# Loading a merge's inverse blocks ahead of its other inputs, in a fused attention and DeltaNet layer

## The chip, the cores and the metric

The kernel runs on one core of a Trainium2 chip. The metric is the time of one execution on the device in microseconds (us). Inside the core, TensorE (PE) multiplies matrices and transposes, VectorE (DVE), ScalarE (ACT) and GpSimd (POOL) work elementwise, and SyncE (SP) issues most transfers between the chip's memory and the on-chip buffers. Each engine takes its instructions strictly in program order; they meet at semaphores.

## The reference, cut to what matters

One layer of a diffusion backbone mixes 1024 latent tokens (and 256 context tokens) in two ways side by side: neighbourhood attention with 8 heads, and a bidirectional gated DeltaNet with 4 heads. The change is in the DeltaNet's preparation. For each chunk of tokens and each direction it needs the inverse of a unit triangular matrix:

```python
a = jnp.where(pos[:, None] > pos[None, :],
              jnp.einsum('nbhid,nbhjd->nbhij', kb, k) * decay, 0.0)
t_inv = lax.linalg.triangular_solve(eye + a, jnp.broadcast_to(eye, a.shape),
                                    left_side=True, lower=True, unit_diagonal=True)
u = jnp.einsum('nbhij,nbhje->nbhie', t_inv, v * beta[..., None])
```

The inverses are then used in a scan over the chunks. The kernel uses chunks of 128 tokens, so 10 chunks (2 context, 8 latent), 2 directions and 4 heads: 80 triangular matrices of 128 x 128.

## The kernel before, in words

The kernel has two phases. In the first (to about 552 us), all projections of the inputs run on TensorE, with the preparation of the DeltaNet spread among them; in the second, attention and the scan run interleaved, and then the output projection.

**Inverting in blocks.** A 128 x 128 triangular matrix is cut into four diagonal blocks of 32. For each head, `delta_front` computes the triangular matrices (`pm`), stores them to memory (`pm_dram`, one tensor per head), and copies their diagonal blocks, from memory to memory, to `ab_dram` (line 1046), one block per row. `inv_groups` loads 120 such rows at a time (the last group, number 2, has 80: line 1055, tile `ab_vv`), and `inv_blocks` inverts them on VectorE in 31 steps of two instructions (lines 1078 and 1081). The inverted blocks go back to memory as `yd` (line 1087). Groups 0 and 1 hold heads 0, 1 and most of head 2; group 2 holds the rest of head 2 and head 3.

**Merging.** `inv_merge` puts one head's inverse together, in turns that are separated by `yield`:

- turn l: load `pm` of the head (two loads `pmf`, one per direction, line 1095), and the inverted blocks (four loads `vl`, line 1106, 20 rows each);
- turn t: three VectorE transposes, `vx`, `vd`, `ld` (lines 1114 to 1116), and four ScalarE copies into `tm` (line 1120);
- turn z: 40 small matmuls `tz` of `pmf` and `ld` (line 1128), ScalarE copies `zt` (line 1132), more copies into `xo` and `tm`;
- turn u: 60 small matmuls `tu` (line 1147) and six VectorE copies (line 1152);
- turns w and e: the same once more for blocks of 64 (lines 1161 to 1172), and the store of the result `tm` to `tm_dram` (line 1174).

The turns of the four heads follow the list `MERGES`, "0l 0t 1l 0z 0u 1t 0w 2l 0e ...". Two buffers `vl` serve heads 0, 2 and heads 1, 3; `pmf` too has one pair of buffers for the even heads (in the pool `pf`, tags `kk0`, `kk1`) and one for the odd. `tm` has one buffer per parity for direction 0, and one, `tms[2]`, that all heads share for direction 1.

**What sets the order.** A scheduler orders each engine's instructions from the program's order, priorities and dependencies. `phase_a2` takes turns between the remaining projections (`self.fill`) and two generators: `blocks`, which inverts group 2 and then loads the attention's first inputs, and `merges`. Turns of `merges` run with the priority raised by 200, the first turn of `blocks` by 300. `self.order(r, name)` adds a pure order between two instructions.

**SyncE's ring.** Each transfer that SyncE issues takes one of eight semaphores in turn, and waits for the transfer that used it last, eight places earlier. While a transfer waits, everything behind it in SyncE's queue waits too.

**Projections.** They have three PSUM buffers, taken in turn. A result is split by ScalarE and VectorE into a high and a low part (`sh`, `sl`, lines 527 to 531), which are stored to `qk_dram` from a ring of four buffers (lines 532, 533). In the listings, `pk2_1` is the second half of k of the third pair of attention heads, `pz2_0` a half of its gate, `pq3_0` a half of q of the fourth pair.

Of the kernel before, what the change touches and what calls it, by code (L numbers as in the profile page):

```python
# [11 lines left out]
F32 = mybir.dt.float32  # L12
# [8 lines left out]
P = 128  # L21
# [120 lines left out]
class K:  # L142
# [946 lines left out]
    def inv_merge(self, g3, ps, h):  # L1089
        nc = self.nc  # L1090
        pm = []
        for d in range(2):
            pool, tag = (g3, f"pm{d}") if h % 2 else (self.pf, f"kk{d}")
            pm.append(pool.tile([P, 10, P], F32, name=f"pmf{h}_{d}", tag=tag))
            nc.sync.dma_start(pm[d][0:96], self.pm_dram[h][0:96, d])
        if h == 0:

            self.vls = [self.pf.tile([P, S], F32, name=f"vl{i}", tag=f"q{c}") for i, c in enumerate(("l0", "h1"))]
# [4 lines left out]
        vl = self.vls[h % 2]  # L1103
        for b in range(4):
            g, i = divmod(8 * h + 2 * b, 12)
            nc.sync.dma_start(vl[32 * b:32 * b + 20], self.yd[g][10 * i:10 * i + 20].rearrange("t j i -> t (j i)"))
        vd, ld = (g3.tile([P, 2, 10, 32], F32, name=f"{c}d{h}", tag=f"{c}d", bufs=2) for c in "vl")

        xo = self.xo
        tm = [self.tms[h % 2], self.tms[2]]  # L1110
        yield
        vx = self.pf.tile([P, S], F32, name=f"vx{h}", tag="ql1")
        flat = lambda w: w.rearrange("p d t c -> p (d t c)")
        nc.vector.transpose(vx, vl)
# [25 lines left out]
        for d in range(2):  # L1140
            pu = ps.tile([P, 10, 32], F32, name=f"tu{h}_{d}", tag="tb", bufs=2)
            where = [(r, r + c - 1) for r in (1, 3) for c in (0, 1) if (r, c) != ((3, 1), (1, 0))[d]]
            for t in range(10):
                for r, c in where:
                    s2, sc = slice(32 * r, 32 * r + 32), slice(32 * c, 32 * c + 32)
                    a, b = (zt, vd) if c < r else (vd, zt)
# [293 lines left out]
    def phase_a2(self):  # L1440
        tc, ps = self.tc, self.ps
        with tc.tile_pool(name="a2", bufs=1, side="right", reuse_waits="tile") as ap:
            ready = self.ready
            buf = lambda nm, tag, n: self.pf.tile([P, n], F32, name=f"{nm}_{tag}", tag=tag)

            def blocks():
                vv = buf("ab", "vv", 2 * S)
                yield from self.inv_groups((2,), lambda nm, n: buf("tb2", "qh0", n) if n < S else vv[:, :S] if "ab" in nm
                                           else vv[:, S:])
                self.mk = self.pf.tile([P, MTOT], mybir.dt.bfloat16, name="mk")  # L1450
                self.load(self.mk, self.I["masks"])
                while len(ready) < 4:
                    yield
                self.na_pairs = {0: self.na_load(None, 0)}
                yield

            def merges():

                heads = [self.inv_merge(ap, ps, h) for h in range(4)]
                for c in MERGES.split():  # L1460
                    h = int(c[0])
                    while c[1:] == "l" and (8 * h + 7) // 12 not in self.yd:
                        yield
                    next(heads[h])
                    if c[1:] == "e":
                        ready.append(h)
                    yield

            pr, gens = self.fill, (blocks(), merges())
            credit = [0.0, 0.0]  # L1470
            first = True
            for _ in range(3):
                next(pr)
            for _ in pr:
                for i, (g, r) in enumerate(zip(gens, (3, 3))):
                    credit[i] += r
                    while credit[i] > 0:
                        if i:
                            with tc.high_priority(offset=200):
                                next(g, None)  # L1480
                        elif first:
                            first = False
                            with tc.high_priority(offset=300):
                                next(g, None)
                        else:
                            next(g, None)
                        credit[i] -= 1
            for g in gens:
                for _ in g:
                    pass  # L1490
# [66 lines left out]
```

## Time and profile before

| | before |
|---|---|
| median of 3 runs | 872.3 us (871.33 to 875.08) |
| profiled execution, its time | 871.71 us |
| its span, first to last instruction | 869.9 us |
| mean granted clock of TensorE | 0.972 |
| PE busy | 824.9 us, 95% of the span |
| DVE busy | 502.7 us, 58% |
| ACT busy | 417.3 us, 48% |
| POOL busy | 357.3 us, 41% |
| SyncE's and ScalarE's transfers (q1, hardware queue) | 144.94 MB, 53% of the 16 engines' span |

How to read it: all times are counted from the first instruction of the span. A row of the timeline has the start, the length, the engine, the line, the operation, `out<-in` by the program's names (heads and buffer numbers left out, so `vl` is either buffer and `pmf` any head's), and in brackets the idle time of the engine just before it with what ended it. "SPq" rows are the issuing of transfers; their length is the time of issue, not of the transfer. In a row of stretches, PE's busy share counts time at a low clock as busy, so the granted clock stands beside it. Matmuls overlap in the pipeline: their pitch is read from their starts.

### The profile page before, as it was taken

To read this page: it belongs to the slowest core of one execution; us is meant where nothing else is said; L and a number is where in the kernel's file an instruction comes from. 1 tells how busy PE (TensorE), PEld (TensorE's weight loads), DVE (VectorE), ACT (ScalarE), POOL (GpSimd) and SP (SyncE) were. 2 spreads that over 40 slices of the span, in tenths; PEclk is the share of its full clock that TensorE was granted. 3 is DMA by queue.
4 is the path that set the end of the run, shared out by engine and by line. 5 is a ranking of instruction groups with operands and counts; after the bars stand their busy time and mean duration, and the time that the engine had idled before them with its cause. 6 is when DMAs were issued, how large, how long until landed. Compare 5 with 4: busy or idle time off the path is not lost.

```text
span 869.9 us, 16461 instructions
## 1 busy us (share of the span) xinstructions
PE 824.9 (95%) x6082; PEld 696.4 (80%) x6082; DVE 502.7 (58%) x1051; ACT 417.3 (48%) x1087; POOL 357.3 (41%) x430
## 2 busy tenths in 40 slices
PE   6999999999999989989898999899999999999996
PEld 3678887888788867769786788788898988878885
DVE  3444455536743699859935964456666655653342
ACT  5244334753664643355314334366666667734210
POOL 2224141453462553328262100655757559624110
PEclk9999999999999999989998999699999999999999
DMA  8778352255444825562597569995967925134251
GB/s 340 265 259 295 97 170 88 73 170 168 142 157 154 221 85 170 176 171 81 176 283 226 160 187 290 419 258 149 313 179 262 259 78 191 49 110 133 87 184 69
DMA packets 86054, 159.65 MB, mean 184 GB/s; under 512 B 18373, under 2 KB 45334, under 8 KB 83798
## 3 DMA queue, kind: packets, MB, share of 16 engines
q1 hardware_dynamic: 78486, 144.94, 53.0%
q10 hardware_dynamic: 7488, 13.67, 5.1%
q8 instruction: 48, 0.79, 0.4%
q14 instruction: 32, 0.26, 0.1%
HBM read 109.51 MB, written 52.42 MB: 186 GB/s over the span
## 4 chain that ended last, share of the span: by engine, by line
PE 59%; DVE 16%; DMA 15%; issue 4%; ACT 2%; POOL 2%; SPq 1%; DVEq 0%; POOLq 0%; ACTq 0%
PE py L1369 3%; PE py L1370 3%; PE py L1371 3%; DVE tb L1078 3%; DVE vb L1081 3%; PE pa L1260 2%; PE pz L463 2%; PE pz L468 2%; PE pz L467 2%; PE po L789 2%; DMA wada<-in_w_ada 2%; PE pa L1271 2%; PE po L784 2%; DMA pm_dram<-pm 2%; PE tr L772 2%
## 5 line engine op out<-in xcount | busy, mean ns | idle before, releaser
L759 ACT ACTIVATE pt<-pt,nm 128x544 f32<-128x544 f32 (+1 forms) x64 | 50.5, 790 | 37.5 <-DVE nm L758 37.0
L758 DVE CUSTOM_DVE_ANT_0 pt<-sc,gm 128x544 f32<-128x544 f32 (+1 forms) x64 | 49.4, 771 | 32.2 <-PE sc L754 25.8
L742 POOL TENSOR_TENSOR gm<-gt,mk 128x288 f32<-128x288 f32 (+1 forms) x48 | 46.5, 971 | 29.1 <-DVE nm L758 28.8
L1232 POOL TENSOR_SCALAR kd<-kt,kd 128x128 f32<-128x128 f32 x72 | 42.7, 605 | 20.5 <-PE pa L1271 19.9
L1020 ACT ACTIVATE em<-em,gc 128x128 f32<-128x128 f32 x80 | 25.5, 391 | 34.9 <-DMA em<-gc_dram 29.7
L467 PE MATMUL pz<-hl,wh_gz 128*128 128x512 f32 x96 | 38.6, 402 | 0.0
L463 PE MATMUL pz<-hh,wh_gz 128*128 128x512 f32 x96 | 38.3, 399 | 0.0
L468 PE MATMUL pz<-hh,wl_gz 128*128 128x512 f32 x96 | 38.2, 398 | 0.0
L476 PE MATMUL pv<-wh_nv,hh 128*128 128x264 f32 x128 | 35.5, 296 | 2.0 <-ACT hh L265 1.7
L477 PE MATMUL pv<-wh_nv,hl 128*128 128x264 f32 x128 | 36.8, 292 | 0.0
L1431 DVE TENSOR_TENSOR finv<-py,ggb 128x512 f32<-128x512 f32 x16 | 10.9, 689 | 43.2 <-ACT finv L1430 43.1
L478 PE MATMUL pv<-wl_nv,hh 128*128 128x264 f32 x128 | 35.6, 287 | 0.0
L1274 DVE SCALAR_TENSOR_TENSOR s<-s,egl,pa 128x128 f32<-128x128 f32 x64 | 19.6, 344 | 27.2 <-PE pa L1271 27.2
L1039 POOL TENSOR_SCALAR_AFFINE_SELECT qe<-qe 128x256 f32<-128x256 f32 x32 | 25.5, 800 | 24.1 <-DVE qe L1038 24.1
L887 DVE SCALAR_TENSOR_TENSOR acc_v<-xp_v,cols,acc_v 128x1282 f32<-128x1282 f32 x16 | 29.1, 1817 | 10.9 <-ACT acc_v L885 10.6
L1078 DVE TENSOR_TENSOR tb<-ab,vb 120x31 f32<-120x31 f32 (+15 forms) x62 | 30.2, 487 | 8.7 <-DMA ab<-ab_dram 7.1
L1137 POOL COPY tm<-ld 32x320 f32<-32x320 f32 x16 | 7.4, 464 | 65.0 <-DMA tm_dram<-tm 27.1
L1430 ACT ACTIVATE finv<-py 128x512 f32<-128x512 f32 x16 | 9.5, 597 | 48.6 <-PE py L1371 30.5
L1238 POOL TENSOR_SCALAR vb<-v,beta 128x128 f32<-128x128 f32 x40 | 24.2, 604 | 20.4 <-DVE y L1244 17.2
L772 PE MATMUL tr<-c,pt 128*96 128x128 f32 (+1 forms) x192 | 31.8, 275 | 0.0
L1035 DVE SCALAR_TENSOR_TENSOR pm<-pk,beta,em 128x128 f32<-128x128 f32 x80 | 23.5, 342 | 14.0 <-PE pk L1028 10.9
L770 ACT COPY tcx<-tc 128x256 f32<-128x256 f32 x64 | 23.4, 366 | 16.2 <-PE tc L768 15.8
(432 smaller groups left out, 2852.7 us busy)
## 6 DMA issues: line engine op xcount, KB each, us to landing
wada<-in_w_ada SPq DMA_DIRECT2D x16, 512.0 KB
em<-gc_dram SPq DMA_DIRECT2D x20, 256.0 KB
pm_dram<-pm SPq DMA_DIRECT2D x20, 256.0 KB
tm_dram<-tm SPq DMA_DIRECT2D x8, 640.0 KB
kk<-qk_dram SPq DMA_DIRECT2D x16, 320.0 KB
tm<-tm_dram SPq DMA_DIRECT2D x4, 1280.0 KB
kq_dram<-kq SPq DMA_DIRECT2D x4, 1152.0 KB
kq<-kq_dram SPq DMA_DIRECT2D x4, 1152.0 KB
```

The source lines that it names most:

```text
L463: r = nc.tensor.matmul(ps, wh, xh, start=(k == 0), stop=False)
L467: nc.tensor.matmul(ps, wh, xl, start=False, stop=False)
L468: nc.tensor.matmul(ps, wl, xh, start=False, stop=(k == KC - 1))
L476: nc.tensor.matmul(ps, xh, wh, start=(k == 0), stop=False)
L477: nc.tensor.matmul(ps, xl, wh, start=False, stop=False)
L478: nc.tensor.matmul(ps, xh, wl, start=False, stop=(k == KC - 1))
L742: r = nc.gpsimd.tensor_tensor(self.gm[hh][:, 384 - n:384].rearrange("p (n c r) -> p n c r", c=nco, r=4), gv, self.mk[:, mo:mo + n].rearran ...
L758: nc.vector.tensor_tensor_reduce(pt[:, 384 - n:], sc[:, 512 - n:768], gm[:, 384 - n:], -1.0, 3.0e38, ALU.add, ALU.min, nm)
L759: self.last_exp = nc.scalar.activation(pt[:, 384 - n:], pt[:, 384 - n:], AF.Exp, bias=nm, scale=-1.0, accum_out=sums[:, ct, hh:hh + 1]).in ...
L772: self.pe(nc.tensor.transpose(pl[:m, rc * P:(rc + 1) * P], pt[:, 384 + (rc - 3) * m:384 + (rc - 2) * m], self.ident))
L1078: nc.vector.tensor_tensor(t3, bc(ab[:, 0:m, m:m + 1], [r, m, n]), bc(vb[:, m:m + 1, m:], [r, m, n]), ALU.mult)
L1232: r = nc.gpsimd.tensor_scalar(kd[d], kt_[:, t, :], self.kd[:, h, d, t:t + 1], None, ALU.mult)
```

## The change

In `inv_merge`, the two `pmf` loads go into a function `others()`. It is called behind the `vl` loads, at the end of turn l, and for head 1 at the beginning of turn t. Each `pmf` load is ordered behind the last of the head's `vl` loads. In `phase_a2`, the first turn of `merges` (head 0's turn l) is taken before all else there, with a priority raised by 600.

```diff
     def inv_merge(self, g3, ps, h):
         nc = self.nc
         pm = []
-        for d in range(2):
-            pool, tag = (g3, f"pm{d}") if h % 2 else (self.pf, f"kk{d}")
-            pm.append(pool.tile([P, 10, P], F32, name=f"pmf{h}_{d}", tag=tag))
-            nc.sync.dma_start(pm[d][0:96], self.pm_dram[h][0:96, d])
+
+        def others():
+            for d in range(2):
+                pool, tag = (g3, f"pm{d}") if h % 2 else (self.pf, f"kk{d}")
+                pm.append(pool.tile([P, 10, P], F32, name=f"pmf{h}_{d}", tag=tag))
+                self.order(nc.sync.dma_start(pm[d][0:96], self.pm_dram[h][0:96, d]), block)
         if h == 0:
...
         vl = self.vls[h % 2]
         for b in range(4):
             g, i = divmod(8 * h + 2 * b, 12)
-            nc.sync.dma_start(vl[32 * b:32 * b + 20], self.yd[g][10 * i:10 * i + 20].rearrange("t j i -> t (j i)"))
+            block = nc.sync.dma_start(vl[32 * b:32 * b + 20], self.yd[g][10 * i:10 * i + 20].rearrange("t j i -> t (j i)")).ins.name
...
         tm = [self.tms[h % 2], self.tms[2]]
+        if h != 1:
+            others()
         yield
+        if h == 1:
+            others()
...
             first = True
+            with tc.high_priority(offset=600):
+                next(gens[1])
             for _ in range(3):
                 next(pr)
```

How the order moves is seen at three places. Lines of the changed kernel are 2 to 8 higher. The first is SyncE's queue behind the copy of head 3's diagonal blocks to `ab_dram`, before (the number behind a name's underscore is an instruction's; `pmf1_0` is head 1, direction 0):

```order
L1046 DMA ab_dram_94<-pm_dram3_76 32x20x32 x4
L1095 DMA pmf0_0_4383<-pm_dram0_73 96x1280
L1095 DMA pmf1_0_4413<-pm_dram1_74 96x1280
L1095 DMA pmf0_1_4385<-pm_dram0_73 96x1280
L1095 DMA pmf1_1_4415<-pm_dram1_74 96x1280
L1055 DMA ab_vv_4368<-ab_dram_94 80x1024
L1106 DMA vl1_4388<-yd0_3389 20x1024 x2
L1106 DMA vl1_4388<-yd1_4175 20x1024 x2
L1106 DMA vl0_4387<-yd0_3389 20x1024 x4
L532 DMA qk_dram_93<-sh_k22_4460 128x256
L533 DMA qk_dram_93<-sl_k22_4461 128x256
```

and with the change:

```order
L1046 DMA ab_dram_94<-pm_dram3_76 32x20x32 x4
L532 DMA qk_dram_93<-sh_k22_4511 128x256
L533 DMA qk_dram_93<-sl_k22_4512 128x256
L1108 DMA vl0_4184<-yd0_3389 20x1024 x4
L1097 DMA pmf0_0_4202<-pm_dram0_73 96x1280
L1097 DMA pmf0_1_4204<-pm_dram0_73 96x1280
L1055 DMA ab_vv_4390<-ab_dram_94 80x1024
L1108 DMA vl1_4185<-yd0_3389 20x1024 x2
L1108 DMA vl1_4185<-yd1_4175 20x1024 x2
L1097 DMA pmf1_0_4603<-pm_dram1_74 96x1280
L1097 DMA pmf1_1_4605<-pm_dram1_74 96x1280
L1108 DMA vl0_4184<-yd1_4175 20x1024 x4
```

The k stores and head 0's blocks move ahead of everything; ab_vv has two big loads before it instead of four; head 2's blocks (the last row) follow at once.

The second is ScalarE around head 0's copies, before (`wh` rows are weight casts, `st_z` a gate activation):

```order
L448 CAST wh_nq3_0_5186<-wr_nq3_0_5185 128x512
L448 CAST wh_nq3_4_5192<-wr_nq3_4_5191 128x512
L446 DMA wr_nk3_4_5533<-in_w_in 128x512
L446 DMA wr_gz3_0_5632<-in_w_in 128x512
L527 ACTIVATE sh_k21_4758<-pk2_1_4733 128x512
L555 ACTIVATE st_z20_4948<-pz2_0_4923 128x512
L1120 COPY tm0_4389<-vd0_4403 32x10x32 x4
L1136 COPY xo_4392<-vd0_4403 32x10x32 x2
L1136 COPY xo_4392<-ld0_4404 32x10x32 x2
```

and with the change:

```order
L448 CAST wh_nq3_0_5215<-wr_nq3_0_5214 128x512
L1126 COPY tm0_4186<-vd0_4200 32x10x32 x4
L1142 COPY xo_4189<-vd0_4200 32x10x32 x2
L1142 COPY xo_4189<-ld0_4201 32x10x32 x2
L448 CAST wh_nq3_4_5221<-wr_nq3_4_5220 128x512
L527 ACTIVATE sh_k21_4813<-pk2_1_4788 128x512
L446 DMA wr_nk3_4_5533<-in_w_in 128x512
L1126 COPY tm1_4187<-vd1_4417 32x10x32 x4
L1138 COPY zt0_4419<-tz0_0_4420 32x320 x2
L1138 COPY zt0_4419<-tz0_1_4443 32x320 x2
L446 DMA wr_gz3_0_5632<-in_w_in 128x512
L555 ACTIVATE st_z20_4977<-pz2_0_4952 128x512
```

Head 0's copies move ahead of a cast and two activations, and the copies of head 1's blocks (`tm1<-vd1`) stand directly ahead of head 0's `zt`.

The third is TensorE, where `tz` of head 0 now comes after 17 of the 48 gate matmuls `pz2` and its `tu` after 39 of them (before: after all 48, and 1 and 21 more of `pq3_0`). Further on, at the last merge step of head 0, before (`tu20_00` and `tu20_10` use the same two PSUM buffers as `tu20_05` and `tu20_15`):

```order
L1167 MATMUL tu20_00_4703<-tm0_4389,z20_4664 64x64
L1169 MATMUL tu20_10_4704<-z20_4664,xo_4392 64x64
L1161 MATMUL tz20_15_4686<-tm2_4391,pmf0_1_4385 64x64 x5
L1128 MATMUL tz1_0_4781<-ld1_4422,pmf1_0_4413 32x32 x20
L1128 MATMUL tz1_1_4804<-ld1_4422,pmf1_1_4415 32x32 x14
L1167 MATMUL tu20_05_4717<-tm0_4389,z20_4664 64x64 x5
```

and the last rows of that piece with the change:

```order
L1134 MATMUL tz1_0_4734<-ld1_4418,pmf1_0_4603 32x32 x11
L1134 MATMUL tz1_1_4757<-ld1_4418,pmf1_1_4605 32x32 x20
L467 MATMUL pq3_1_5410<-hl_113,wh_nq3_0_5215 128x512
L468 MATMUL pq3_1_5410<-hh_112,wl_nq3_0_5216 128x512
...
L463 MATMUL pk3_2_5539<-chh_114,wh_nk3_0_5528 128x256
L1173 MATMUL tu20_05_4717<-tm0_4186,z20_4615 64x64
```

17 projection matmuls of `pq3_1` and one of `pk3_2` (most are left out here) now stand between `tz1` and `tu20_05`.

## Prediction

> **What bounds the kernel now.** I read the page first, then busy time by stretches, then TensorE's waits, and last what SyncE, VectorE and ScalarE do around those waits.
>
> ```profile
> PE 824.9 (95%) x6082; PEld 696.4 (80%) x6082; DVE 502.7 (58%) x1051; ACT 417.3 (48%) x1087; POOL 357.3 (41%) x430
> ...
> 560.00:860.00 300.00, 292.13 (x2327) 256.75 (x2326) 163.51 (x451) 162.41 (x480) 151.19 (x204) 1.00 0.58 174
> ```
>
> TensorE (PE) is busy 95% of the span, and in the second phase (from 560 us on) 292.1 of 300 us at the full granted clock. The change touches nothing there, so whatever the merges end earlier or later, the kernel ends about that much earlier or later. The merges run from 452 to 552 us. By stretches of 5 us (columns: PE, PEld, DVE, ACT, POOL busy, granted clock, DMA share, GB/s):
>
> ```profile
> 465.00:470.00 5.00, 1.83 (x25) 0.99 (x25) 4.60 (x7) 2.56 (x5) 0.42 (x1) 0.98 0.91 274
> 470.00:475.00 5.00, 5.00 (x76) 4.26 (x72) 4.91 (x8) 4.86 (x12) 2.75 (x5) 0.50 0.69 234
> 475.00:480.00 5.00, 5.00 (x123) 3.91 (x124) 3.00 (x6) 2.56 (x6) 1.27 (x1) 0.84 0.57 186
> ...
> 490.00:495.00 5.00, 3.21 (x105) 2.89 (x103) 4.79 (x12) 1.45 (x4) 0.95 (x1) 1.00 0.74 206
> 495.00:500.00 5.00, 4.66 (x44) 4.42 (x45) 4.64 (x12) 1.74 (x4) 0.00 (x0) 0.71 0.78 259
> 500.00:505.00 5.00, 5.00 (x136) 4.01 (x135) 4.60 (x12) 2.21 (x5) 1.95 (x4) 0.95 0.56 210
> ```
>
> Two holes in PE, and each is followed by a stretch at a lower clock, in which PE is "busy" and does half the work. The holes themselves, in TensorE's timeline (start, length, and the idle time before it with its releaser):
>
> ```profile
> 454.55 0.40 PE L463 MATMUL pz<-hh,wh_gz 128*128 128x512 f32 x1
> ...
> 465.50 0.40 PE L468 MATMUL pz<-hh,wl_gz 128*128 128x512 f32 x1
> 467.45 0.51 PE L463 MATMUL pq<-hh,wh_nq 128*128 128x512 f32 x1 [1.56 <-DVE sl_k L529]
> 469.57 2.22 PE L1128 MATMUL tz<-ld,pmf 32*32 32x32 f32 x80 [1.61 <-DVE ld L1116]
> ...
> 495.34 0.79 PE L1167 MATMUL tu<-tm,z 64*64 64x64 f32 x10 [2.13 <-DVE tm L1171]
> ```
>
> What they cost: idle 1.56 + 1.61 = 3.2 us, then clock 0.98, 0.50 and 0.84 over three stretches of 5 us: 0.1 + 2.5 + 0.8 = 3.4 us lost. The second hole: 2.1 us, then 0.71 and 0.95: 1.45 + 0.25 = 1.7 us. Together **10.4 us** that better order could win back in this piece, and no more.
>
> **Where the first hole comes from.** SyncE's queue:
>
> ```profile
> 448.21 1.97 SPq L1095 DMA_DIRECT2D pmf<-pm_dram  x4
> 451.28 0.30 SPq L1055 DMA_DIRECT2D ab_vv<-ab_dram  x1
> 451.62 11.08 SPq L1106 DMA_DIRECT2D vl<-yd  x8
> 462.81 0.34 SPq L532 DMA_DIRECT2D qk_dram<-sh_k  x1
> ...
> 455.77 0.27 SPq L1106 DMA_DIRECT2D vl<-yd  x1
> 458.06 0.27 SPq L1106 DMA_DIRECT2D vl<-yd  x1
> 460.55 0.27 SPq L1106 DMA_DIRECT2D vl<-yd  x1
> 462.44 0.27 SPq L1106 DMA_DIRECT2D vl<-yd  x1
> ```
>
> Four big loads (pmf, 480 KB each, heads 0 and 1) go out at 448.2; the eight small vl loads behind them take 11.1 us to be issued, since each waits for the transfer eight places before it. So the last four vl issues mark landings: pmf by pmf, then ab_vv at 462.44. From 451.28 to 460.55 four pmf landed, 2.3 us each; ab_vv, 320 KB, took 1.9. The k stores behind them leave only at 462.81, and the pq projections at 467.45 wait for the buffers that hang on them.
>
> ```profile
> 462.51 0.20 DVE L1078 TENSOR_TENSOR tb_qh<-ab_vv 80x31 f32<-80x31 f32 x1 [11.92 <-DMA ab_vv<-ab_dram]
> 465.40 1.25 DVE L1114 STREAM_TRANSPOSE vx<-vl 128x1024 f32<-128x1024 f32 x1 [1.07 <-DMA qk_dram<-sl_k]
> 467.32 1.26 DVE L1115 STREAM_TRANSPOSE vd<-vx 128x640 f32<-128x640 f32 x1
> 468.68 0.83 DVE L1116 STREAM_TRANSPOSE ld<-vd 128x640 f32<-128x640 f32 x1
> 476.93 1.25 DVE L1114 STREAM_TRANSPOSE vx<-vl 128x1024 f32<-128x1024 f32 x1 [1.99 <-DMA vl<-yd]
> 510.51 0.19 DVE L1081 TENSOR_TENSOR ab_vv<-ab_vv,tb_qh 80x31 f32<-80x31 f32 x1
> ...
> 472.89 1.85 ACT L1120 COPY tm<-vd 32x320 f32<-32x320 f32 x4
> 475.91 1.75 ACT L1132 COPY zt<-tz 32x320 f32<-32x320 f32 x4
> ```
>
> VectorE idles 11.9 us, then is nearly full until the last inversion step (510.5). That inversion feeds head 3, so VectorE is a second chain behind TensorE's.
>
> **The change, part by part.** No instruction is added that computes; the order moves.
>
> *New order of the transfers.* Behind the band stores, which have landed at 451.3: two k stores, vl of head 0, its two pmf, ab_vv, vl of head 1, its two pmf, vl of head 2. I price them in a row: the k pair (256 KB) 1.2 us at the pmf rate of 480 KB in 2.3 us. A vl group (320 KB in four transfers) has no clean row. From below: 1.5 us at the pmf rate. From above, the chain of waits:
>
> ```profile
> 472.48 4.33 DMA vl<-yd
> ```
>
> I take 2.3 us, near the 1.9 that ab_vv needs for the same bytes. Landings: vl0 at 454.8, pmf0 at 459.4, ab_vv at 461.3 (462.4 before), vl1 at 463.6, pmf1 at 468.2, vl2 at 470.5.
>
> [...]
>
> *First hole, anew.* TensorE meets tz of head 0 after 17 of the 48 pz matmuls: their pitch is (465.50 - 454.55)/47 = 0.233 us, so at 458.5. VectorE has transposed by 454.8 + 1.25 + 1.26 + 0.83 = 458.1, but pmf0 is there at 459.4: 0.9 us of waiting. At the full clock the two tz groups take
>
> ```profile
> 516.63 1.45 PE L1128 MATMUL tz<-ld,pmf 32*32 32x32 f32 x80
> ```
>
> so until 460.9, and 22 more pz matmuls until 466.0. Then come the tu matmuls of head 0, and here the order has a trap: their input zt is copied on ScalarE behind the four tm copies of *head 1*, which need head 1's vl. vl1 463.6, vx 1.25, one inversion step 0.3, vd 1.27: 466.4; tm 1.85: 468.2; half of zt 0.9: 469.1. TensorE waits 3.1 us. Queued behind this on TensorE: the rest of pz and all of pq; behind the tm copies on ScalarE: the gate activation and the next weight casts, which have slack of several us. So the new hole is 0.9 + 3.1 = 4.0 us against 3.2: the wait for head 0's vl goes, and the wait for head 1's takes its place. tu comes at 469 and not behind pq near 479 mainly because it now stands ahead of 30 matmuls that it followed before (9 pz and 21 pq); that is order, not gain.
>
> *Clock after it.* Before, 3.2 and 2.1 us of idling were followed by 3.4 and 1.7 us lost. I take 2.6, the middle.
>
> *Second hole.* tu20_05 waited for VectorE to empty the two PSUM buffers of tu20_00/10; only 39 small matmuls stood between. Now 17 projection matmuls are added there, 17 x 0.233 = 4.0 us against the wait of 2.1. VectorE must also be in time:
>
> ```profile
> 495.31 0.49 DVE L1172 TENSOR_SCALAR tm<-tu 64x320 f32<-64x320 f32 x1
> ```
>
> From head 2's vx (476.93) to the end of this step it took 18.9 us, with about as many inversion steps between as now: 470.5 + 18.9 = 489.4. TensorE gets to tu20_05 at 469.1 + 1.45 (tu, taken as tz) + 58 x 0.233 (projections) + some 4.8 (the other small groups, an estimate from tz's 1.45) + 2.6 (clock) = 491.5. So I count the hole and its 1.7 us as gone; if VectorE is 4 us later than that, the hole is back.
>
> *Sum.* 10.4 before, 4.0 + 2.6 = 6.6 now: **3.8 us less**. Can it reach the end? VectorE: ab_vv 1.1 us earlier, head 0's three transposes (3.3 us) now in front of the inversion, in time that was idle; its idle 1.07 + 1.99 is replaced by waits for vl1 (463.6 - 462.3) and vl2 (470.5 - 468.7), also 3.1. So the inversion ends 4.4 us earlier, which covers 3.8. Later on, heads 2 and 3 meet
>
> ```profile
> 532.06 0.48 DVE L1152 TENSOR_SCALAR tm<-tu 32x320 f32<-32x320 f32 x1 [3.59 <-DMA tm_dram<-tm]
> ...
> 534.02 0.62 PE L1161 MATMUL tz<-tm,pmf 64*64 64x64 f32 x7
> ...
> 539.37 6.80 DMA tm_dram<-tm
> ...
> 552.45 0.72 PE sc L751 x2
> ```
>
> the store of head 1's result, which follows from that inversion, with 1.5 us in hand on TensorE (532.06 + 0.48 to 534.02); and the store of head 2's, 6.8 us, which moves along.
>
> Bounds: with vl groups at 1.5 us, the hole is 0.1 + 2.3 and the clock may cost 1.7: gain 6.3. At 4.33 us: vl0 456.8, pmf0 461.4 (wait 2.9), vl1 467.6, tu at 473.1 for a TensorE ready at 468.0 (wait 5.1), clock 3.4: 11.4, a loss of 1.0.
>
> **How it stands to the times.** The profiled execution took 871.71 us (span 869.9 and 1.8 around it); the median of the three runs is 872.3, 0.6 above. 3.8 off the median: 868.5.
>
> **The rivals.**
>
> *The trap doesn't close* (865.5). vl1 lands by 461 or the clock stays up. The holes shrink to 2.4 and no loss after: 8.0 less on TensorE, with VectorE's chain (4.4 to 6.8 earlier, plus the 1.5 us in hand) capping it near 7. For it: not every hole is followed by a low clock:
>
> ```profile
> 417.09 0.41 PE L944 MATMUL tb<-c,tok 128*128 128x128 f32 x2 [2.86 <-DVE tok L921]
> ...
> 400.00:420.00 20.00, 17.14 (x143) 16.96 (x142) 19.07 (x38) 7.70 (x33) 13.45 (x8) 1.00 0.30 82
> ```
>
> 2.86 us idle there and the clock stayed at 1.00. Against it: 2.13 us at 495 did cost. [...]
>
> *The gain is spent at the seam* (872). The merges' end and the attention's first loads (540 to 560) run at a low clock anyway; two more such windows (1.7 each) take 3.4 of the 3.8. For it: head 2's store took 6.8 us among those loads. Against: the loads' order there is unchanged.
>
> *Slower* (877): one mechanism, the vl loads. They now stand at the head of the chain, and TensorE and ScalarE have their dependents early in their queues. At 4.33 us a group the holes are 2.9 and 5.1; if both are followed by the longer loss (3.4 each), 14.8 against 10.4: 4.4 slower, 876.7 and up. It decides from about 4 us a group. Against it: ab_vv's 1.9 for the same bytes, and that the 4.33 held an issue wait and other loads.
>
> That the reorder doesn't take place is excluded: the orders in the part on the change show it.
>
> **How the numbers follow.** Forecast 0.45 (868.5, its own range 866 to 871); trap doesn't close 0.27; seam 0.17; slower 0.11. Changes under 0.5%, 4.4 us, can't be told from none here: faster is below 867.9, slower above 876.7. Faster: 0.26 of the second case and 0.19 of the forecast's, 0.45. Slower: most of the last, 0.10. Same: 0.45. The range of 8 in 10: 863.5 to 876.5, from just below the better rival to the edge of the worse.
>
> **What would show it.** Right: the first vx (L1114) at about 455; ab_vv landing near 461; TensorE's first tu (L1147) near 469, after a hole of some 3 us whose releaser is ScalarE's zt (L1132), with VectorE's vd and the vl loads behind it; no hole before tu (L1167) near 490; last inversion step near 506; the attention's first sc (L751) near 548.6 (552.4 before). Wrong: a hole before tu under 1 us or over 6; a clock below 1.00 in more than two stretches of 5 us between 458 and 505; an sc that moves by another amount than the total.

## The result, and the profile after

The changed kernel takes 879.54 us (median of five runs, 878.79 to 882.02) against 872.74 (871.33 to 875.15): a ratio of **1.0091, 95% interval 1.0071 to 1.0111**, some 7.9 us slower. The forecast was 868.5 us with a range of 863.5 to 876.5 and a chance of 0.10 for slower. The profiled execution took 878.79 us, its span is 876.7 (869.9 before).

The first line of the page already says where to look (busy time, share, instructions of PE and PEld, then the other engines):

```profile
PE 832.5 (95%) x6082; PEld 702.9 (80%) x6082; DVE 505.2 (58%) x1051; ACT 418.0 (48%) x1087; POOL 357.9 (41%) x430
```

The same number of matmul records, 6082, keeps TensorE busy 7.6 us longer (832.5 against 824.9), while its idle time fell from 45.0 to 44.2 us. So the loss is not a wait. It is work that got slower.

First the places that the prediction named, in VectorE's and TensorE's timelines (start, length, and the idle time ahead with its releaser):

```profile
454.34 1.25 DVE L1120 STREAM_TRANSPOSE vx<-vl 128x1024 f32<-128x1024 f32 x1 [3.24 <-POOL wl_nq L449]
460.66 0.20 DVE L1078 TENSOR_TENSOR tb_qh<-ab_vv 80x31 f32<-80x31 f32 x1 [2.81 <-DMA ab_vv<-ab_dram]
462.96 1.25 DVE L1120 STREAM_TRANSPOSE vx<-vl 128x1024 f32<-128x1024 f32 x1 [1.34 <-DMA vl<-yd]
509.39 0.18 DVE L1081 TENSOR_TENSOR ab_vv<-ab_vv,tb_qh 80x31 f32<-80x31 f32 x1
...
459.10 1.45 PE L1134 MATMUL tz<-ld,pmf 32*32 32x32 f32 x80
467.97 0.21 PE L1153 MATMUL tu<-vd,zt 32*32 32x32 f32 x1 [2.10 <-ACT zt L1138]
...
558.52 0.58 PE L751 MATMUL sc<-kk,qh 128*128 128x256 f32 x1
```

Head 0's blocks are transposed at 454.3 (465.4 before), the inversion's load is in use at 460.7 (462.5 before), head 1's blocks at 463.0, and `tu` follows at 468.0 behind a hole that ScalarE's `zt` ends. Up to here the kernel runs as forecast. But the attention's first `sc` comes at 558.5, where 548.6 was forecast and 552.4 was the time before. Of the 6.8 us that the span grew, 6.1 are there by `sc`.

By stretches of 5 us (columns: PE, PEld, DVE, ACT, POOL busy, granted clock, DMA share, GB/s), after:

```profile
465.00:470.00 5.00, 2.65 (x124) 1.93 (x122) 3.23 (x8) 3.49 (x8) 0.00 (x0) 1.00 0.83 249
470.00:475.00 5.00, 5.00 (x25) 3.93 (x17) 4.79 (x10) 2.33 (x4) 1.91 (x2) 0.66 0.98 321
...
485.00:490.00 5.00, 5.00 (x60) 3.80 (x61) 4.61 (x11) 0.40 (x1) 0.00 (x0) 0.74 0.71 218
490.00:495.00 5.00, 5.00 (x58) 4.18 (x53) 4.06 (x10) 2.29 (x5) 0.98 (x1) 0.58 0.15 45
...
515.00:520.00 5.00, 5.00 (x52) 3.74 (x50) 0.48 (x1) 0.42 (x1) 0.00 (x0) 0.81 0.96 234
520.00:525.00 5.00, 5.00 (x70) 4.26 (x71) 3.55 (x4) 2.27 (x5) 0.00 (x0) 0.51 1.16 244
```

and three of these before, which the prediction did not need:

```profile
485.00:490.00 5.00, 5.00 (x48) 4.17 (x47) 4.86 (x8) 3.20 (x7) 1.17 (x2) 1.00 0.00 0
...
515.00:520.00 5.00, 5.00 (x127) 4.04 (x126) 1.58 (x3) 2.69 (x6) 0.00 (x0) 1.00 0.84 201
520.00:525.00 5.00, 5.00 (x28) 3.90 (x29) 4.32 (x5) 0.91 (x2) 0.00 (x0) 1.00 1.16 250
```

The first hole and the clock behind it are smaller than before (2.3 us of idling and 5 x 0.34 = 1.7 of clock). But there are two new stretches at a low clock, 485 to 495 and 515 to 525, with PE "busy" throughout: 1.3 + 2.1 = 3.4 us lost in the first, 0.95 + 2.45 = 3.4 in the second.

TensorE's timeline at the head of the first one shows what it was doing (the 40 `tz` matmuls leave 80 records, so x2 is one matmul here):

```profile
484.56 0.27 PE L1173 MATMUL tu<-tm,z 64*64 64x64 f32 x1
...
484.88 0.24 PE L1134 MATMUL tz<-ld,pmf 32*32 32x32 f32 x2
485.05 0.33 PE L1175 MATMUL tu<-z,xo 64*64 64x64 f32 x2
485.30 0.24 PE L1134 MATMUL tz<-ld,pmf 32*32 32x32 f32 x2
485.48 0.33 PE L1173 MATMUL tu<-tm,z 64*64 64x64 f32 x2
...
487.69 0.47 PE L1175 MATMUL tu<-z,xo 64*64 64x64 f32 x2
488.09 0.31 PE L1134 MATMUL tz<-ld,pmf 32*32 32x32 f32 x2
488.33 0.47 PE L1173 MATMUL tu<-tm,z 64*64 64x64 f32 x2
...
491.21 0.80 PE L467 MATMUL pq<-hl,wh_nq 128*128 128x512 f32 x1
```

In the kernel before, the same matmuls:

```profile
490.87 0.22 PE L1167 MATMUL tu<-tm,z 64*64 64x64 f32 x1
490.92 0.22 PE L1169 MATMUL tu<-z,xo 64*64 64x64 f32 x1
490.93 0.22 PE L1167 MATMUL tu<-tm,z 64*64 64x64 f32 x1
...
491.94 1.26 PE L1128 MATMUL tz<-ld,pmf 32*32 32x32 f32 x68
```

The change makes the scheduler deal the `tu` matmuls of head 0 (64x64) and the `tz` matmuls of head 1 (32x32) out in turn: behind the first `tu` one `tz` and one `tu`, nine times, and then the other 31 `tz` in a run. That is 19 changes of size where runs need one, and the same comes again for heads 1 and 2 at 515. One pair, a `tu` and a `tz`, takes 485.48 - 485.05 = 0.43 us. In runs, the ten `tu` take about 0.7 us: `tu20_00` and `tu20_10` are both 64x64, at different places of the array, and where they alternate two records come every 0.06 us in the rows of before. In the first experiment below all ten take 0.73 us (484.50 to 485.23), no more than the five `tu20_05` alone (488.78 to 489.50, 0.72). 80 `tz` records take 1.45, so a matmul is 0.04. A pair in runs is 0.07 + 0.04 = 0.11 us, and going over to the other size and back costs 0.32: **0.16 us a switch**, 2.9 us for the 18 that are too many. From 487.69 on the pair takes 0.64 us (488.33 - 487.69): the clock has fallen (granted 0.88 between 487.0 and 487.5, 0.50 behind that). From 484.15, the start of the last tz20 group, to the next projection at 491.21 the piece takes 7.0 us; the same matmuls in runs take about 2.6 (2.7 in the kernel before, 515.33 to 518.01; 2.5 in the first experiment below).

### The profile page after: what moved, and what is told of

The parts are those of the page before. It is cut to its first block, busy times and chain, and to the rows that moved or that the text cites. A ratio compares the mean times of both kernels' runs of the same rounds, so it can differ in the third digit from the quotient of the medians.

```text
span 876.7 us, 16463 instructions
## 1 busy us (share of the span) xinstructions
PE 832.5 (95%) x6082; PEld 702.9 (80%) x6082; DVE 505.2 (58%) x1051; ACT 418.0 (48%) x1087; POOL 357.9 (41%) x430
## 4 chain that ended last, share of the span: by engine, by line
PE 71%; DVE 13%; DMA 9%; issue 2%; ACT 2%; POOL 1%; SPq 1%; DVEq 0%; POOLq 0%; ACTq 0%
PE py L1375 3%; PE py L1376 3%; PE py L1377 3%; DVE tb L1078 3%; PE pz L467 3%; PE pz L463 3%; PE pz L468 3%; PE pa L1266 2%; DVE vb L1081 2%; PE po L789 2%; PE pa L1277 2%; PE sc L754 2%; PE po L784 2%; PE tr L772 2%; DMA vl<-yd 2%
## 5 line engine op out<-in xcount | busy, mean ns | idle before, releaser
L449 POOL TENSOR_TENSOR wl_gz<-wr_gz,wh_gz 128x512 fp32r<-128x512 f32 x12 | 16.5, 1374 | 37.3 <-ACT wh_gz L448 32.1
```

## The experiments

Theory A: the back and forth between the two sizes costs the time, by itself and by the low clock it brings about. Theory B: the new order of the loads costs it. Theory C: it is lost at the seam to the attention phase. The study has twelve runs. The pieces of code are shortened to what each one orders, and their comments were added here.

### One size in runs, loads as in the changed kernel

```diff
+mm = nc.tensor.matmul(pz[s2, t, :], pm[d][s1, t, s2], ld[s1, d, t, :], ...)   # tz of head h
+if h:
+    self.order(mm, self.tu2_last[h - 1])   # behind the tenth tu matmul of the head before
```

> The changed kernel with the same order of transfers; only the 32x32 tz matmuls of the next head are ordered behind the ten 64x64 tu matmuls of the head before (tu20_00 and tu20_10, and so on for each head), so that TensorE no longer goes back and forth between the two sizes. Theory A (the back and forth is what costs: in the changed kernel the stretch from tz20_15 to the end of tz1 took 484.2 to 491.2 = 7.0 us, against 2.6 us for the same matmuls in runs before, twice, and each is followed by 6.8 us at half clock = 3.4 us lost): the two stretches fall to about 2.7 us each, the low clock behind them goes, up to 2 x (4.4 + 3.4) = 15.6 us less than 879.5; but tu20_05 now stands only 40 tz and 6 projections (about 2.8 us) behind tu20_10, so a wait for VectorE of 1 to 2 us and a low clock of 1.7 can come back: 864 to 871 us. Theory B (the loads: the earlier tz0 and the new waits at 460 and 466 unsettle the clock, the back and forth only shows up as busy time that would otherwise be waiting): no faster than 876. Theory C (the gain and more is lost at the seam to the attention phase, 540 to 567): the stretches at 484 and 515 shrink, but the total stays at 874 or above.

Measured: 869.15 us, **0.9971 of before, interval 0.9949 to 0.9993**. TensorE's timeline and two stretches:

```profile
468.23 0.21 PE L1155 MATMUL tu<-vd,zt 32*32 32x32 f32 x1 [2.56 <-ACT zt L1140]
...
484.50 0.27 PE L1175 MATMUL tu<-tm,z 64*64 64x64 f32 x1
...
485.23 1.45 PE L1134 MATMUL tz<-ld,pmf 32*32 32x32 f32 x80
488.78 0.79 PE L1175 MATMUL tu<-tm,z 64*64 64x64 f32 x10 [0.47 <-DVE tm L1182]
548.52 0.58 PE L751 MATMUL sc<-kk,qh 128*128 128x256 f32 x1
```

```profile
490.00:495.00 5.00, 5.00 (x88) 4.23 (x89) 4.70 (x11) 2.13 (x4) 1.18 (x1) 1.00 0.44 164
...
520.00:525.00 5.00, 5.00 (x36) 3.78 (x34) 1.81 (x4) 3.58 (x8) 1.80 (x4) 1.00 1.06 245
```

The ten `tu` start at 484.50 and are followed by `tz` at 485.23, the 40 `tz` matmuls take 1.45 us again, the clock stays at 1.00 at both places, and `sc` is at 548.5, 10.0 us ahead of the changed kernel's. The merges' loads up to there, and the hole before `tu` that they lead to (2.56 us), are as in the changed kernel. Theories B and C fall.

### One of the two left in

```diff
-if h:
+if h > 1:
     self.order(mm, self.tu2_last[h - 1])
```

> As the first kernel, but the back and forth between heads 0 and 1 (484 to 491 us) is left as it was; only those behind it are put into runs. Theory A: about half of the gain of the first kernel is gone, that is 4.4 us of switching and up to 3.4 us of clock: 6 to 8 us slower than the first kernel, 870 to 876 us. Theory B and C: the same time as the first kernel, within 2 us.

Measured: 873.9 us, 1.0023 (0.9998 to 1.0049), by the ratios 4.5 us slower than the first kernel: between B's and C's "within 2" and A's "6 to 8", nearer to A, and within A's 870 to 876. The clock falls behind the piece that was left, and not at the other:

```profile
490.00:495.00 5.00, 5.00 (x19) 3.88 (x14) 4.37 (x9) 1.50 (x4) 1.44 (x1) 0.50 0.02 4
...
520.00:525.00 5.00, 5.00 (x100) 4.01 (x102) 3.37 (x5) 0.91 (x2) 0.00 (x0) 1.00 1.16 234
```

### The back and forth put into the kernel before

```diff
+if h in (1, 2):   # tz of head h, before's order of loads
+    k = min(20 * d + 2 * t + b // 2, 9)
+    self.order(mm, self.tu2s[k].ins.name)
+    if k < 9:
+        self.order(self.tu2s[k + 1], mm.ins.name)
```

> The kernel before, with its own order of transfers; only ten tz matmuls of the next head are placed one by one between the ten tu matmuls of tu20_00/tu20_10, and the same for tu21, the back and forth that the changed kernel has. Theory A: the two stretches take about 7 us against 2.6, and the clock falls behind them: 8.8 to 15.6 us slower than 872.7, less up to 3.8 us because 19 projections then stand in front of tu20_05 and its wait (2.1 us, and 1.7 us of clock) goes: 878 to 888 us. Theory B and C: the loads are those of before, so the time is that of before, 870 to 875 us.

Measured: 902.14 us, 1.0354 (1.0310 to 1.0399). The direction is A's, but 30 us is far more than A's 5 to 15. The waits between 545 and 600 (engine, line, what for, us in total, times, longest) tell why:

```profile
PE tz L1167 <- DVE xo L1158: 21.7, 1, 21.7
DVE tm L1158 <- DMA tm_dram<-tm: 20.1, 1, 20.1
```

The new order of the matmuls made the scheduler also put head 2's two `tm` stores behind seven attention loads on SyncE. That is a side effect, and this run can't be used for the price of the switches. (The expectations reckon with 0.14 us a switch, since they take a `tu` matmul in a run at 0.11 us instead of 0.07, and with 20 switches a piece where the rows have 19.)

### The same, with the stores in their old place

```diff
+self.order(r, self.store2)          # loads of heads 0 and 1 behind head 2's tm stores
+self.order(zg_load, self.scan_loads)
```

> The third kernel once more (before, with the tz and tu20/tu21 matmuls of two sizes one by one), but on SyncE the attention's loads are ordered behind head 2's tm stores again, as they stand in the kernel before; in the third kernel those stores had come behind seven loads and VectorE waited 20.1 us for one of them. Theory A: what is left of the 30.7 us is the back and forth: two stretches of 20 switches at (0.43 - 0.15)/2 = 0.14 us, 5.6 us, and low clock behind each (1.7 to 3.4 us, twice), against the hole before tu20_05 that goes (2.1 us and 1.7 of clock): 3 to 9 us slower than before, 875 to 881 us. Theory E (the third kernel was slow for the stores alone and the back and forth costs nothing): 868 to 873 us.

Measured: 886.44 us, 1.0174 (1.0147 to 1.0201). Again A's direction, and again too much: A had 875 to 881. The second of the two lines, meant to keep `zg` from going ahead, put it too far back. TensorE's wait for it in the attention phase, here and in the kernel before:

```profile
PE ot L1332 <- DVE zg L1336: 4.8, 2, 2.5
```

```profile
PE ot L1319 <- DVE zg L1323: 0.8, 1, 0.8
```

### Nine switches instead of nineteen

```diff
-k = min(20 * d + 2 * t + b // 2, 9)
+k = min(5 + 20 * d + 2 * t + b // 2, 9)
```

> As the sixth kernel, with only four of the ten tu matmuls of each of the two stretches placed one by one between tz matmuls: 9 switches instead of 20. Theory A, switches alone: 0.14 us each, 1.3 us a stretch instead of 2.8, about 3 us less than the sixth kernel, and stretches of some 3.9 us from the first tu to the last tz. If the low clock behind them needs a long stretch of switching (the ones seen began 4.3 to 6 us after the first switch), it goes as well and the time comes to 870 to 874 us; if a short one is enough, it stays and the time is 873 to 877 us.

Measured: 881.3 us, 1.0137 (1.0097 to 1.0178), above both of A's ranges: it carries the same wait for `zg` (5.1 us). By the ratios it is 3 us less than with nineteen, the size of A's price, but the two intervals overlap, so this pair of runs doesn't show the price. (In the traces of the changed, the second, the sixth and the eighth kernel the clock falls 1.9 to 4.1 us after the first of nineteen switches, where the expectation has 4.3 to 6.)

### Both once more, with zg where the kernel before has it

```diff
-self.order(zg_load, self.scan_loads)
+self.order(zg_load, self.kq1)        # behind head 1's kq
```

> The sixth kernel with one side effect taken out: there the load of zg, which the output projection's first turn waits for, had come behind all loads of head 1 (TensorE waited 4.8 us for zg against 0.8 in the kernel before, and a stretch at half clock followed); now it stands behind head 1's kq, as in the kernel before. What is left against before is the back and forth between 64x64 and 32x32 matmuls, twice with 20 switches. Theory A: 20 x 0.14 = 2.8 us of switching, twice, and 6.8 us at half clock (3.4 lost) behind each, less the hole before tu20_05 (2.1) and its clock (1.7): 5.6 + 6.8 - 3.8 = 8.6 us slower than before, 878 to 884 us. Theory E (the back and forth costs nothing, side effects made the third and sixth kernels slow): 870 to 874 us.

> The seventh kernel (9 switches in each of the two stretches) with the load of zg in its old place. In the seventh kernel's trace no low clock stands behind the two short stretches, and TensorE waited 5.1 us for zg. Theory A with the clock falling only behind a long stretch of switching: 2 x 9 x 0.14 = 2.5 us for the switches, less the hole before tu20_05 and its clock (3.8): 869 to 875 us. If a short stretch is enough to bring the clock down: 875 to 879 us.

Measured: with nineteen switches **879.5 us, 1.0090 (1.0073 to 1.0108)**, 7.8 us slower than before where 8.6 was worked out; with nine 872.39 us, 1.0018 (0.9998 to 1.0039), within A's 869 to 875 and 6.3 us less than with nineteen. TensorE's wait for `zg` is 0.8 us in both, as before. So the kernel before becomes as slow as the changed one when it is given the back and forth. Each of these edits also moves some later stores and loads on SyncE, but the two kernels differ only in the number of switches that is asked for, and the one with nine bounds what the added orders cost by themselves. The clock behind the first piece, nineteen switches:

```profile
490.00:495.00 5.00, 5.00 (x84) 4.05 (x83) 3.85 (x9) 0.83 (x2) 0.00 (x0) 0.51 0.37 128
495.00:500.00 5.00, 5.00 (x18) 4.42 (x19) 2.21 (x6) 1.22 (x3) 0.00 (x0) 0.50 0.16 52
```

and nine, in the two kernels that have them (first the one with `zg` misplaced, then the mended one):

```profile
490.00:495.00 5.00, 5.00 (x120) 4.33 (x120) 4.76 (x11) 1.95 (x5) 0.15 (x1) 1.00 0.65 189
```

```profile
490.00:495.00 5.00, 5.00 (x39) 4.25 (x33) 3.33 (x9) 0.96 (x3) 0.00 (x0) 0.50 0.61 199
```

With the same order of matmuls there, the short piece left the clock alone in one profiled execution and brought it down in the other. (That second one took 876.86 us, among the longest of its kernel, whose times spread from 869.4 to 878.0.) So the expectation's "only behind a long stretch" doesn't hold: a short one was enough in one of these two executions, and not in the other.

### The hole before tu taken away

The first kernel still waits 2.56 us before `tu`, the trap of the prediction. Here ScalarE's copies of head 1 are put behind head 0's `zt` (and each head's `tu20_05` behind the next head's `tz`, which keeps the runs whole):

```diff
-cp(tm[0][sl, :, sl], vd[sl, 0])
+c0 = cp(tm[0][sl, :, sl], vd[sl, 0])
+if h == 1:
+    self.order(c0, self.zt0)
```

> The first kernel of the study (matmuls of one size in runs), and on ScalarE the four tm copies of head 1 are ordered behind head 0's zt copies, so that tu of head 0 no longer waits for head 1's blocks. The first kernel's trace has that wait as 2.56 + 0.19 us before tu (468.23, released by ScalarE's zt) and then one stretch of 3.4 us at half clock (1.7 us). Theory A (the wait is what the prediction called the trap, and it is paid in full): both go, 4.4 us less than the first kernel's 869.15, 864.8, less if the gain meets another wait: 864 to 867 us. Theory D (the time is taken up later, by VectorE's inversion or by head 2's store and the low clock from 540 on): 868 to 871 us, with tu at about 465 and the attention's first sc no earlier than 547.

Measured: 871.09 us, 0.9986 (0.9965 to 1.0007), no better than the first kernel. `tu` now runs at 464.2 without a wait, and then:

```profile
475.51 0.47 DVE L1163 TENSOR_SCALAR tm<-tu 32x320 f32<-32x320 f32 x1
...
476.53 1.75 PE L1172 MATMUL tz<-xo,pmf 64*64 64x64 f32 x14 [5.93 <-DVE xo L1163]
```

VectorE takes `tu` out of PSUM ten us later, since head 2's transpose and five inversion steps stand ahead. The wait moved by one engine and doubled. So VectorE's copies of `tu` were ordered ahead as well:

```diff
+self.order(step27, ev)      # inversion step m = 27 behind head 0's tu copies
+self.order(vx2, self.tu0)   # head 2's first transpose too
```

> The fifth kernel (one size in runs, head 0's zt copies first on ScalarE), and on VectorE the six copies of head 0's tu out of PSUM are ordered ahead of head 2's first transpose and of the inversion step behind head 1's transposes. In the fifth kernel tu was done at 465.7, but these copies stood behind head 2's transpose (which waited 2.32 us for its blocks) and four inversion steps and ran at 475.5 to 479, so that TensorE waited 5.93 us at 470.6 and ran at half clock for 10.2 us behind. Theory A with the trap's price coming free: neither hole nor low clock between 458 and 530, 4.4 us less than the first kernel: 862 to 867 us. Theory D (the next wait takes it, at head 2's store or at 540): 868 to 872 us.

Measured: 871.87 us, 1.0006 (0.9984 to 1.0028). The hole shrank to 1.60 us, but the time is not better. Part of the gain went at once: the granted clock behind the hole was 0.87, 0.50 and 0.94 in three stretches of 5 us, some 3.4 us lost, where the first kernel lost 1.7. The last projection ended at 535.9, only 0.7 us earlier than there. Behind it, on TensorE and on VectorE:

```profile
541.92 0.37 PE L1184 MATMUL tz<-xo,pmf 64*64 64x64 f32 x2 [4.81 <-issue]
546.45 2.07 PE L1184 MATMUL tz<-tm,pmf 64*64 64x64 f32 x17 [3.11 <-POOL tm L1154]
...
545.33 0.48 DVE L1169 TENSOR_SCALAR tm<-tu 32x320 f32<-32x320 f32 x1 [1.47 <-DMA tm_dram<-tm]
```

What was left is spent where head 3's merge stands alone, with no projection left to fill in, as theory D has it. The last attempt brings head 2's stores forward on SyncE:

```diff
+self.order(later_store, self.store2)   # one k and two z stores behind head 2's tm stores
```

> The tenth kernel (head 0's wait and the hole behind it gone, projections done by 535.4) with head 2's two tm stores ahead of three other stores on SyncE (one of k, two of z). In the tenth kernel they were issued at 536.3, though VectorE had finished head 2 at 531.5, and head 3's work waited for them until 545.4 (TensorE 4.8 and 3.1 us). If what ate the gain is the place of these stores in SyncE's queue: first sc at 547 to 549 instead of 551.5, and 866 to 869.5 us. If it is the load on the DMA queues at that time, whatever stands first: 870 to 873 us.

Measured: 870.13 us, 0.9976 (0.9958 to 0.9994), no better than the first kernel on the same chip (0.9970, below). The stores were issued at 532.1 instead of 536.3, and the second of the waits fell from 3.11 to 1.79, but the first stayed:

```profile
542.05 0.37 PE L1194 MATMUL tz<-xo,pmf 64*64 64x64 f32 x2 [5.16 <-issue]
545.27 2.07 PE L1194 MATMUL tz<-tm,pmf 64*64 64x64 f32 x17 [1.79 <-POOL tm L1164]
```

So the stores' place was at most a small part. What TensorE waits for at 537 to 542, between two matmuls of one group and with nothing recorded, stays open.

### The first kernel again

> The first kernel of the study once more, beside the eleventh on the same chip and against other executions of the kernel before: 0.995 to 0.999 of before (0.9971 was measured). If that gain was of its chip only: 1.000 and above.

Measured: 869.87 us, **0.9970 (0.9956 to 0.9985)**. The gain of the new loads, with each size in runs, holds on another chip. This version, the change with its matmuls kept in runs of one size, is faster than both kernels, by 2.6 us against the one before and by some 10.5 against the changed one.

## Why the prediction was wrong

**The landings and the first hole: right.** vx 454.3 (forecast 454.8), ab_vv 460.7 (461.3), vl1 463.0 (463.6), `tu` at 468.0 (469.1) behind ScalarE's `zt`, with head 1's copies ahead of it. `pmf0` landed in time for `tz` at 459.10, and head 1's blocks came 0.6 us early, so the hole was 2.3 us and not 4.0; the clock behind it cost 1.7 and not 2.6. The vl loads, on which the slower rival rested, are not the cause.

**The second hole: gone, as said.** VectorE's two steps ran at 488.84 and 489.48 (forecast: done at 489.4), and `tu20_05` met no wait. But it came at 496.88, where the sum had 491.5:

```profile
496.88 0.27 PE L1173 MATMUL tu<-tm,z 64*64 64x64 f32 x1
```

**The step that failed** is the term in that same working: "some 4.8 (the other small groups, an estimate from tz's 1.45)". It prices the small matmuls by their pitch in a run, and the sum has no term for their new order: "No instruction is added that computes; the order moves." The two groups of `tu` and `tz` took 7.0 us each, not 2.6, and 6.8 us at half clock came with each (487.4 to 494.2 and 518.1 to 524.9). The part on the change printed "the last rows of that piece"; the rows directly above those, left out there, are the ones where `tu` and `tz` alternate. The order was known ahead, and its price was not asked for. No row of the trace of before shows such a piece, so it should have been bounded from both sides like the vl loads.

With that term in place the sum closes. Of the 10.4 us lost before, 2.3 + 1.7 remain, and new waits of 0.39 and 0.17 us before tz20 add 0.6: 5.8 gained. The two pieces take 7.0 instead of 2.6, 8.8 lost, with the low clock inside them. Of the 3.4 + 3.4 us of clock about 1.9 and 1.8 lie inside (from the fall to the next projection, 491.21 - 487.4 = 3.8 us at half, and 3.7 at the second piece), so 3.1 come behind: 11.9 lost. That is 6.1 us slower, and the first `sc` came 6.1 later.

What the traces show of the price: 0.16 us where 64x64 and 32x32 meet (a pair takes 0.43 us instead of 0.11), no loss to be seen where 64x64 matmuls at two places alternate (0.73 us for ten, 0.72 for five at one place).

**The rivals.** None of them was this one. "The trap doesn't close" gave 865.5 and the forecast 868.5; with the back and forth taken out, the same loads give 869.15 and 869.87, with `sc` at 548.5 where 548.6 was forecast. So the forecast for the loads was near, and the change contained a second change that had not been priced. That `sc` agrees to 0.1 us is partly luck: the hole there was 2.8 us and not 4.0, the clock cost 1.7 and not 2.6, and three small waits, 1.4 us together, made up most of the difference; by the ratios the loads are worth 2.5 and 2.6 us, not 3.8. The seam rival fits the attempts to improve further: taking the trap away (the fifth, tenth and eleventh kernels) brought nothing to the end, since VectorE's queue, then a longer low clock, and then head 3's lonely merge took it.

**The signs named.** The transposes, ab_vv, `tu` and its releaser, and no hole near 490 came out right. The inversion's end (509.4 for 506) and `sc` were wrong, and both by the same step: VectorE stood still for the slow piece,

```profile
497.71 0.48 DVE L1177 TENSOR_SCALAR tm<-tu 64x320 f32<-64x320 f32 x1 [3.33 <-PE tu L1175]
```

and with the back and forth taken out the inversion ended at 506.6 (506.2 in the repetition). One of the named signs of a wrong prediction appeared: the clock was below 1.00 in three stretches between 458 and 505 (0.66, 0.74, 0.58).

**A part that does nothing.** Holding back head 1's other inputs changes no instruction's place: with `others()` called for all heads in turn l, the order on every engine of the built program is the same. What the change does comes from the ordering behind the blocks and the early first turn. Without that first turn the two sizes stay apart by themselves:

```diff
-with tc.high_priority(offset=600):
-    next(gens[1])
```

> The changed kernel without the turn of head 0 that is taken first at a raised priority. The blocks of head 0 then go out half before and half behind the last load of the inversion, all blocks ahead of all other inputs, and the two sizes stand in runs on TensorE by themselves (tu20 in 3, 1 and 1, then all of tz1). Theory A: no back and forth, no such loss: within 5 us of before, 867 to 875 us, with tz0 about 3 us later than in the changed kernel. Theory B: loads in a new order still cost, 876 us and above.

Measured: 870.35 us, 0.9988 (0.9968 to 1.0007), as A expected. So the early turn brings the alternation with it; ordering the other inputs behind the blocks does not.

## What to carry to other kernels

When a change moves matmuls of different tile sizes, read the new order matmul by matmul and count where one size follows another: a scheduler that takes a switch for free can deal two ready groups out one by one, as here. Keep each size in a run, with an order dependency if need be, and look for the loss in TensorE's busy time, not in its waits. And read the order on every queue after any such edit, for three of the experiments here were spoiled by a store or a load that came to stand elsewhere than meant.

## What the hardware showed that was not expected

- **A switch between 64x64 and 32x32 matmuls cost 0.16 us** at a granted clock of 1.00 (a pair took 0.43 us instead of 0.11; 0.64 us at 0.50). The profile counts it as busy time: 5.00 of 5.00 us in the stretch at 485.
- **The clock fell without a hole.** In the changed kernel PE is busy 5.00 of 5.00 us in the stretches at 485 and 515, and the clock falls at about 487.4, 2.5 us after the first switch (484.88), and at about 518.1, 2.6 us after it (515.46). It fell at both pieces with nineteen switches in the sixth and the eighth kernel too, and at the one in the second, 1.9 us (eighth, first piece) to 4.1 us (eighth, second piece) after the first switch; behind nine switches it fell at both pieces in one execution (0.81 and 0.89 in the stretches at 485 and 515) and at neither in the other (1.00). PE was busy 5.00 of 5.00 us in all these stretches, so no idle time stands in them. What brings the clock down was not measured.
- **A wait without a cause on record.** Within one group of matmuls at the end of the merges, TensorE stood still for 0.5 to 5.2 us ("issue") in the profiles of nine of the thirteen kernels. The DMA share there was 1.04 in the kernel before (540 to 545), 1.05 in the changed one (548 to 552), and 1.05 and 1.03 in the tenth and eleventh (540 to 545). The fifth kernel has the same share (0.98 to 1.03 from 535 to 560) and no such wait, so the share alone doesn't explain it. It is longest in the tenth and eleventh kernels, 4.8 and 5.2 us. Its cause was not looked for.
